# Selective-scan groups of a hybrid decoder block: VectorE order, y_diag order, and the engine of the rstd diagonals

## Chip, core and metric

One core of a Trainium2 chip runs the whole block: TensorE (PE), VectorE (DVE), ScalarE (ACT) and GpSimd (POOL) each work through a queue of their own in order, SyncE (SP) issues most transfers. The metric is the device time of one execution in microseconds (us), the median of three runs. All arithmetic is float32; the large products are made from splits, so that a float32 operand is a rounded high part plus a low part, and one product is three matmuls.

## What is computed

One decoder layer on 512 tokens of width 1024: dilated attention and a Mamba-2 mixer fed by one input projection, merged by gates, then a squared-ReLU MLP. The change is in the mixer. Its eight groups have four heads of 64 channels and a state of 128; the scan is made in four chunks of 128 tokens:

```python
def ssd_chunked(x, dt, a, bmat, cmat):
    ...
    a_cs = jnp.cumsum(la, axis=-1)
    decay = jnp.exp(jnp.where(tril, a_cs[..., :, None] - a_cs[..., None, :], -jnp.inf))
    cb = jnp.einsum('bclgn,bcsgn->bcgls', cc, bc)
    y_diag = jnp.einsum('bcghls,bcsghp->bclghp', cb[:, :, :, None] * decay, xd)
    decay_states = jnp.exp(a_cs[..., -1:] - a_cs)
    states = jnp.einsum('bclgn,bcghl,bclghp->bcghpn', bc, decay_states, xd)
    def step(hstate, inp):
        st, dec = inp
        return hstate * dec[..., None, None] + st, hstate
    _, prev = lax.scan(step, init, (states, chunk_decay))
    y_off = jnp.einsum('bclgn,bcghpn,bcghl->bclghp', cc, prev, jnp.exp(a_cs))
    return y_diag + y_off

def mamba2_mixer(...):
    ...
    y = y + d_skip * xh
    y = y * jax.nn.silu(z)
    y = y * lax.rsqrt(jnp.mean(y * y, axis=-1, keepdims=True) + RMS_EPS)   # over the 256 channels of a group
    y = y * norm_w
```

## The kernel before

The program runs through the attention, then the eight mixer groups (about 244 to 700 us), then the output projection and the MLP. In the mixer stage PE has two kinds of work. The large projections come in units of 256 columns: `x` and `bc` (inputs of the convolution of group g), `z` (its gate), `sp` (the output projection of group g-1, added into eight tiles `acc`), and at the end `gs`. A unit's weights are loaded by SP into `ws`, rounded by ACT into `wh` (L90) and the rest `wl` is taken by DVE (L93), for these units in two halves of four k-steps each; `ws`, `wh` and `wl` have two buffers each, so that a unit's split waits for the end of the last unit but one. PE results go to three banks (`psg`) for the units and five (`psa`) for the scan.

The scan of a group is `ssm_group` (L699), a generator of seven steps. `Filler.run(us)` puts matmuls of the units into PE's queue between two steps, `SSM_FILL = (2, 7, 4, 3, 9, 5, 6)` us of them for each group but the last, which has `SSM_LAST`. The steps: (1) decays `w` and `e`, loaded by a POOL transfer that repeats the cumulated decays on all partitions, then 4 exponentials for `e`, 16 Relus and one large exponential for `w` on ACT (L711 to L715); `xd` and `xs` from transposes; (2) `pb`, `pcb`, the masked `cbm` and four DVE multiplications into `w` (L746); (3) `pst`, the chunk states, and `prev`, the carried states: an ACT copy, and for two further chunks one multiplication and one addition on DVE (L758, L759); (4) for each half j `pyd` (y_diag, 16 rows in a trace), `y` (L771), `pyo` (products with the states, L773), `t1`, sum, gate (L777 to L779), square on ACT (L781), and at the end the sum of the two squares (L784); (5) `pn`, the mean of squares by matmuls, its power by POOL in `rt` (L194, L197), and diagonal matrices `dg` (L793); (6) `rg`, which spreads rstd over the partitions; (7) `yt`, the normalised result, split (L801 to L803).

PE's matmuls stand in the order in which they are written (`mm` pins them). On the other engines a scheduling layer orders the instructions by priority: the place in the code, moved ahead where `high_priority(offset)` is around it; pinned instructions keep their order among themselves. `prep` (L101) issues the next unit's load with offset 300 and splits `x`, `bc`, `z` and `sp` units with offset 0. Evacuations of projections have offset 400.

Of the kernel before, what the change touches and what calls it, by code (L numbers as in the profile page):

```python
# [77 lines left out]
def hybrid_block(ctx: ExitStack, tc: tile.TileContext, a: dict):  # L78
# [22 lines left out]
    def prep(i, offset=300, eng=None):  # L101
        if i >= len(units):
            return
        key, loads, free = units[i]
        with tc.high_priority(offset=offset):
            stage = wpool.tile([P, UF], F32, name=f"ws_{key}", tag="ws", bufs=2)
            for dst, src in loads:
                sp.dma_start(dst(stage), src)
        with tc.high_priority(offset=0 if key.rstrip("0123456789") in ("x", "bc", "z", "sp") or key == "o1" else offset):
            hi = wpool.tile([P, UF], F32R, name=f"wh_{key}", tag="wh", bufs=2)  # L110
            lo = wpool.tile([P, UF], F32R, name=f"wl_{key}", tag="wl", bufs=2)
            if key[:2] in ("up", "dn"):
                split(stage[:, :free], hi[:, :free], lo[:, :free], eng)
            else:
                for f in (slice(0, free // 2), slice(free // 2, free)):
                    split(stage[:, f], hi[:, f], lo[:, f], eng, pinned=key == "o1")
        ready[key] = (hi, lo)

    state = {"next": 0}
# [85 lines left out]
    def pin(ins):  # L205
        return tc.keep_in_program_order(ins)
# [447 lines left out]
    def h64(ap_):  # L654
        return ap_.rearrange("p (q e) -> p q e", e=64)
# [40 lines left out]

    TC = T - P

    def ssm_group(g, sz):  # L699

        xs2 = [convs.pop((g, c)) for c in range(2)]
# [6 lines left out]
        for half in range(2):  # L708
            rs_ = slice(64 * half, 64 * half + 64)
            for j in range(2):  # L710
                act.activation(e[rs_, j, :].rearrange("p (c l) -> p c l", c=3), w5[rs_, half, j, 1:, :], AF.Exp)  # L711

        for r in range(16):
            act.activation(w[:, r, :], w[:, r, :], AF.Relu, scale=-1.0, bias=acs[:, g * 16 + r : g * 16 + r + 1])
        act.activation(w, w, AF.Exp, scale=-1.0)  # L715

        xd = sg.tile([P, NT * UC], F32, name=f"xd{g}", tag="xd")
        for b in range(2):
# [32 lines left out]
        for c in range(3):  # L751
            pv = pst[c // 2][:, (c % 2) * UC : (c % 2 + 1) * UC]
            bs, us = slice(c * P, (c + 1) * P), slice(c * UC, (c + 1) * UC)
            three(pv, bk[0][:, bs], bk[1][:, bs], xsp[0][:, us], xsp[1][:, us], True, True)
        act.activation(prev[:, 0, :], pst[0][:, 0:UC], AF.Copy)
        for c in (1, 2):
            pv = pst[c // 2][:, (c % 2) * UC : (c % 2 + 1) * UC]
            dve.tensor_tensor(h64(prev[:, c, :]), h64(prev[:, c - 1, :]), bc64(cd, g, c, c + 1), op=ALU.mult)  # L758
            dve.tensor_tensor(prev[:, c, :], prev[:, c, :], pv, op=ALU.add)  # L759
        yield  # L760

        ys, sq = [], []
        for j in range(2):
            pyd = abank(f"pyd{g}_{j}")
            for c in range(NT):
                for half in range(2):
                    h = 2 * j + half
                    mm(pyd[64 * half : 64 * half + 64, c * P : (c + 1) * P],
                       xd[:, c * UC + h * 64 : c * UC + (h + 1) * 64], w[:, c * HG + h, :], start=True, stop=True)
            y = sg.tile([P, T], F32, name=f"y{g}_{j}", tag="y", bufs=2)  # L770
            dve.scalar_tensor_tensor(y, xs2[j], dskip[:, 2 * g + j : 2 * g + j + 1], pyd, op0=ALU.mult, op1=ALU.add)  # L771
            pyo = abank(f"pyo{g}_{j}")
            for c in range(1, NT):  # L773
                mm(pyo[:, (c - 1) * P : c * P], prev[:, c - 1, j * P : (j + 1) * P], ct[:, c * P : (c + 1) * P],
                   start=True, stop=True)
# [12 lines left out]
        for c in range(NT):
# [298 lines left out]
```

## Time and profile before

| | |
|---|---|
| Median of 3 runs | 1122.25 us (1120.26 to 1123.79) |
| The profiled execution | 1122.04 us, its span 1120.3 us |
| PE matmuls busy | 1094.8 us, 98% of the span |
| DVE busy | 670.7 us, 60% |
| ACT busy | 482.2 us, 43% |
| Granted TensorE clock, mean | 0.997 |

The span is what the profile shows of the execution; 1.7 us lie around it. Busy shares are over the whole span. In the mixer stage a group takes 54.6 us from one `pn` to the next. A row of the timeline gives start, duration, engine, line, operation and, in brackets, the idle time just before and what ended it.

### The profile page before, as it was taken

Reading aid. Unit: us, or ns where it says so; the run is one execution under the profiler, and the core shown is the slowest. Engines: PE = TensorE matmul, PEld = TensorE weight load, DVE = VectorE, ACT = ScalarE, POOL = GpSimd, SP = SyncE. Lnnn points to the kernel's source line nnn. Section 1 sums busy time; section 2 is a strip of 40 time slices with the busy share of each in tenths; the row PEclk is TensorE's granted clock in tenths of the full one; section 3 lists DMA queues with packets and bytes.
Section 4 is the critical chain, followed back from the end, with each engine's and each line's share of the span. In section 5 each row is a group of like instructions: output and inputs, shape, how many; then the busy total and the mean of one; then the engine's idle time right before and its main releaser. Section 6 shows DMA issues by size and latency. Waiting matters only on the chain.

```text
span 1120.3 us, 13600 instructions
## 1 busy us (share of the span) xinstructions
PE 1094.8 (98%) x5501; PEld 909.5 (81%) x5501; DVE 670.7 (60%) x986; ACT 482.2 (43%) x803; POOL 63.4 (6%) x71
## 2 busy tenths in 40 slices
PE   6999999999999999999999999999999999999997
PEld 6988877778888787878787878889888888888886
DVE  5657665347786869696969685855433234333324
ACT  6256665463556363637272623443322233232321
POOL 2203222000000000000000000000000000000000
PEclk9999999999999999999999999999999999999999
DMA  8232212332333232332323222450332324223212
GB/s 274 77 114 77 69 45 66 104 94 77 112 97 129 76 113 80 108 100 89 113 75 113 76 76 77 187 188 1 113 113 75 113 86 159 102 86 114 75 38 75
DMA packets 86463, 110.86 MB, mean 99 GB/s; under 512 B 4080, under 2 KB 74224, under 8 KB 85376
## 3 DMA queue, kind: packets, MB, share of 16 engines
q1 hardware_dynamic: 85072, 101.01, 28.2%
q0 software_dynamic: 1328, 8.98, 2.1%
q8 instruction: 43, 0.70, 0.3%
q14 instruction: 20, 0.16, 0.0%
HBM read 107.81 MB, written 2.16 MB: 98 GB/s over the span
## 4 chain that ended last, share of the span: by engine, by line
PE 89%; DVE 7%; DMA 2%; issue 1%; ACT 1%; SPq 0%; POOL 0%; POOLq 0%; DVEq 0%; ACTq 0%
PE psu L209 16%; PE psd L209 15%; PE psx L209 8%; PE psbc L209 8%; PE psz L209 8%; PE pssp L209 5%; PE psga L209 4%; PE psgs L209 4%; PE psq L209 3%; PE psk L209 3%; PE psap L209 3%; PE psv L209 3%; PE pq L209 1%; PE po L209 1%; PE pt L212 1%; DVE acc L679 1%
## 5 line engine op out<-in xcount | busy, mean ns | idle before, releaser
L209 PE MATMUL psu<-fh,wh_up 128*128 128x512 f32 (+1 forms) x288 | 105.4, 366 | 0.0
L209 PE MATMUL psu<-fl,wh_up 128*128 128x512 f32 (+1 forms) x288 | 105.2, 365 | 0.0
L209 PE MATMUL psu<-fh,wl_up 128*128 128x512 f32 (+1 forms) x288 | 105.2, 365 | 0.0
L209 PE MATMUL psd<-wl_dn,hh 128*128 128x512 f32 x240 | 93.4, 389 | 0.0
L209 PE MATMUL psd<-wh_dn,hl 128*128 128x512 f32 x240 | 93.4, 389 | 0.0
L209 PE MATMUL psd<-wh_dn,hh 128*128 128x512 f32 x240 | 93.4, 389 | 0.0
L93 DVE TENSOR_TENSOR wl_up<-ws_up,wh_up 128x2048 fp32r<-128x2048 f32 x16 | 36.7, 2292 | 77.6 <-ACT wh_up L90 77.5
L93 DVE TENSOR_TENSOR hl<-hidden,hh 128x512 fp32r<-128x512 f32 x32 | 21.9, 693 | 77.3 <-ACT hh L90 77.2
L90 ACT ACTIVATE hh<-hidden 128x512 fp32r<-128x512 f32 x32 | 20.2, 632 | 103.1 <-PE psd L209 97.6
L209 PEld LDWEIGHTS psu<-fh,wh_up 128*128 128x128 f32 x288 | 54.3, 189 | 8.8
L209 PEld LDWEIGHTS psu<-fh,wl_up 128*128 128x128 f32 x288 | 54.3, 189 | 8.7
L209 PEld LDWEIGHTS psu<-fl,wh_up 128*128 128x128 f32 x288 | 54.3, 189 | 8.7
L90 ACT ACTIVATE wh_up<-ws_up 128x2048 fp32r<-128x2048 f32 x16 | 30.7, 1916 | 61.4 <-PE psu L209 56.1
L209 PEld LDWEIGHTS psd<-wh_dn,hh 128*128 128x128 f32 x240 | 45.0, 188 | 9.5
L209 PEld LDWEIGHTS psd<-wh_dn,hl 128*128 128x128 f32 x240 | 45.0, 188 | 9.4
L209 PEld LDWEIGHTS psd<-wl_dn,hh 128*128 128x128 f32 x240 | 45.0, 188 | 9.3
L209 PE MATMUL psx<-uh,wh_x 128*128 128x512 f32 x128 | 52.4, 410 | 0.0
L209 PE MATMUL psz<-uh,wh_z 128*128 128x512 f32 x128 | 51.1, 399 | 0.0
L209 PE MATMUL pssp<-yth,wh_sp 128*128 128x512 f32 x128 | 51.0, 399 | 0.0
L209 PE MATMUL psbc<-uh,wh_bc 128*128 128x512 f32 x128 | 50.8, 397 | 0.0
L209 PE MATMUL psz<-uh,wl_z 128*128 128x512 f32 x128 | 50.1, 392 | 0.0
L209 PE MATMUL pssp<-yth,wl_sp 128*128 128x512 f32 x128 | 50.1, 392 | 0.0
(271 smaller groups left out, 2792.4 us busy)
## 6 DMA issues: line engine op xcount, KB each, us to landing
ws_up<-in_w_up_dram SPq DMA_DIRECT2D x16, 1024.0 KB, 5.4
ws_dn<-in_w_down_dram SPq DMA_DIRECT2D x15, 1024.0 KB, 5.0
ws_z<-in_w_in_dram SPq DMA_DIRECT2D x8, 1024.0 KB, 5.2
ws_x<-in_w_in_dram SPq DMA_DIRECT2D x8, 1024.0 KB, 5.2
w<-acs_d POOLq DMA_DIRECT2D x8, 1024.0 KB, 5.0
ws_bc<-in_w_in_dram SPq DMA_DIRECT2D x16, 512.0 KB, 4.7
ws_sp<-in_w_ssm_proj_dram SPq DMA_DIRECT2D x8, 1024.0 KB, 4.8
ws_ga<-in_w_in_dram SPq DMA_DIRECT2D x4, 1024.0 KB, 5.3
```

What stands on the lines that cost most here:

```text
L90: ins = act.activation(hi, src, AF.Copy)
L93: (eng or dve).tensor_tensor(lo, src, hi.bitcast(F32), op=ALU.subtract)
L209: tc.keep_in_program_order(pe.matmul(*args, **kw))
L212: tc.keep_in_program_order(pe.transpose(dst, src, ident))
L679: dve.tensor_tensor(acc[o], acc[o], ps, op=ALU.add)
```

## The change

Five edits, all for the mixer stage. The carried states `prev` are put 200 places ahead on ACT and DVE, and their four DVE instructions pinned. The split of the `x` unit (all but the first) is held back (`held`) until the states are written, and its low halves are pinned, so that they stand behind the states in DVE's queue. Both `pyd` halves are issued ahead of the two `pyo`. The decays of group g+1 (`decays`) are written at the end of step 4 of group g, pinned on ACT; the squares are pinned too. The diagonals `dg` are made by four ACT copies with a scale in place of one DVE multiplication.

```diff
+        if key[0] == "x" and key != "x0":
+            held.append(lambda: split_unit(key, stage, free, eng, 0, True))
+        else:
+            split_unit(key, stage, free, eng,
+                       0 if key.rstrip("0123456789") in ("x", "bc", "z", "sp") or key == "o1" else offset)
...
-        (eng or dve).tensor_tensor(lo, src, hi.bitcast(F32), op=ALU.subtract)
+        ins = (eng or dve).tensor_tensor(lo, src, hi.bitcast(F32), op=ALU.subtract)
+        if lo_pinned:
+            tc.keep_in_program_order(ins)
...
+    def decays(g):
...
-                act.activation(e[rs_, j, :].rearrange("p (c l) -> p c l", c=3), w5[rs_, half, j, 1:, :], AF.Exp)
+                pin(act.activation(e[rs_, j, :].rearrange("p (c l) -> p c l", c=3), w5[rs_, half, j, 1:, :], AF.Exp))
...
-        act.activation(w, w, AF.Exp, scale=-1.0)
+        pin(act.activation(w, w, AF.Exp, scale=-1.0))
+        ws_e[g] = w, e
+
+    def ssm_group(g, sz):
+
+        xs2 = [convs.pop((g, c)) for c in range(2)]
+        w, e = ws_e.pop(g)
...
-        act.activation(prev[:, 0, :], pst[0][:, 0:UC], AF.Copy)
-        for c in (1, 2):
-            pv = pst[c // 2][:, (c % 2) * UC : (c % 2 + 1) * UC]
-            dve.tensor_tensor(h64(prev[:, c, :]), h64(prev[:, c - 1, :]), bc64(cd, g, c, c + 1), op=ALU.mult)
-            dve.tensor_tensor(prev[:, c, :], prev[:, c, :], pv, op=ALU.add)
+        with tc.high_priority(offset=200):
+            act.activation(prev[:, 0, :], pst[0][:, 0:UC], AF.Copy)
+            for c in (1, 2):
+                pv = pst[c // 2][:, (c % 2) * UC : (c % 2 + 1) * UC]
+                pin(dve.tensor_tensor(h64(prev[:, c, :]), h64(prev[:, c - 1, :]), bc64(cd, g, c, c + 1), op=ALU.mult))
+                pin(dve.tensor_tensor(prev[:, c, :], prev[:, c, :], pv, op=ALU.add))
+        while held:
+            held.pop()()
         yield
...
+        pyds = [abank(f"pyd{g}_{j}") for j in range(2)]
         for j in range(2):
-            pyd = abank(f"pyd{g}_{j}")
             for c in range(NT):
                 for half in range(2):
                     h = 2 * j + half
-                    mm(pyd[64 * half : 64 * half + 64, c * P : (c + 1) * P],
+                    mm(pyds[j][64 * half : 64 * half + 64, c * P : (c + 1) * P],
                        xd[:, c * UC + h * 64 : c * UC + (h + 1) * 64], w[:, c * HG + h, :], start=True, stop=True)
+        for j in range(2):
             y = sg.tile([P, T], F32, name=f"y{g}_{j}", tag="y", bufs=2)
...
-            act.activation(q, y, AF.Square, scale=1.0 / math.sqrt(UC))
+            pin(act.activation(q, y, AF.Square, scale=1.0 / math.sqrt(UC)))
...
+        if g + 1 < GROUPS:
+            decays(g + 1)
         yield
...
-        dve.tensor_tensor(dg, ident.unsqueeze(1).broadcast_to([P, NT, P]), rt.unsqueeze(2).broadcast_to([P, NT, P]),
-                          op=ALU.mult)
+        for c in range(NT):
+            with tc.high_priority(offset=100):
+                act.activation(dg[:, c, :], ident, AF.Copy, scale=rt[:, c : c + 1])
```

What that makes of the queues is shown for group 2 (names carry the group: `w2`, `prev2`; `wl_x3` and `wl_bc3` are weight splits of group 3; line numbers are those of the kernel the rows are of). Groups 3 to 6 read alike. First DVE where the carried states are made, before:

```order
L746 TENSOR_TENSOR w2_3170<-w2_3170,cbm2_3263 128x512 x2
L93 TENSOR_TENSOR wl_x3_3278<-ws_x3_3275,wh_x3_3277 128x1024
L679 TENSOR_TENSOR acc2_2890<-acc2_2890,pssp1_2_3299 128x512
L679 TENSOR_TENSOR acc3_2899<-acc3_2899,pssp1_3_3324 128x512
L93 TENSOR_TENSOR wl_x3_3278<-ws_x3_3275,wh_x3_3277 128x1024
L758 TENSOR_TENSOR prev2_3303<-prev2_3303,cd_92 128x256
L771 SCALAR_TENSOR_TENSOR y2_0_3345<-ct4_3019,dskip_171,pyd2_0_3336 128x512
L759 TENSOR_TENSOR prev2_3303<-prev2_3303,pst2_0_3304 128x256
L758 TENSOR_TENSOR prev2_3303<-prev2_3303,cd_92 128x256
L759 TENSOR_TENSOR prev2_3303<-prev2_3303,pst2_1_3305 128x256
L777 TENSOR_TENSOR t12_0_3351<-pyo2_0_3347,e2_3172 128x384
```

DVE at the same place in the changed kernel:

```order
L764 TENSOR_TENSOR w2_2954<-w2_2954,cbm2_3269 128x512
L777 TENSOR_TENSOR prev2_3303<-prev2_3303,cd_92 128x256
L764 TENSOR_TENSOR w2_2954<-w2_2954,cbm2_3269 128x512
L691 TENSOR_TENSOR acc2_2893<-acc2_2893,pssp1_2_3299 128x512
L778 TENSOR_TENSOR prev2_3303<-prev2_3303,pst2_0_3304 128x256
L691 TENSOR_TENSOR acc3_2902<-acc3_2902,pssp1_3_3330 128x512
L777 TENSOR_TENSOR prev2_3303<-prev2_3303,cd_92 128x256
L778 TENSOR_TENSOR prev2_3303<-prev2_3303,pst2_1_3305 128x256
L93 TENSOR_TENSOR wl_x3_3321<-ws_x3_3281,wh_x3_3320 128x1024 x2
L793 SCALAR_TENSOR_TENSOR y2_0_3360<-ct4_3046,dskip_171,pyd2_0_3342 128x512
L799 TENSOR_TENSOR t12_0_3366<-pyo2_0_3362,e2_2956 128x384
```

The states have moved ahead of the fourth `w`, of two `acc` and of both halves of the `x` split. Then DVE at the end of step 4, up to the sum of squares that `pn` reads, before:

```order
L777 TENSOR_TENSOR t12_1_3372<-pyo2_1_3368,e2_3172 128x384
L679 TENSOR_TENSOR acc5_2960<-acc5_2960,pssp1_5_3383 128x512
L778 TENSOR_TENSOR y2_1_3366<-y2_1_3366,t12_1_3372 128x384
L779 SCALAR_TENSOR_TENSOR y2_1_3366<-y2_1_3366,sz2_1_3272 128x512
L679 TENSOR_TENSOR acc6_2969<-acc6_2969,pssp1_6_3391 128x512
L784 TENSOR_TENSOR sq2_0_3355<-sq2_0_3355,sq2_1_3376 128x512
```

And in the changed kernel:

```order
L691 TENSOR_TENSOR acc7_3005<-acc7_3005,pssp1_7_3429 128x512
L799 TENSOR_TENSOR t12_1_3378<-pyo2_1_3374,e2_2956 128x384
L93 TENSOR_TENSOR wl_bc3_3441<-ws_bc3_3437,wh_bc3_3440 128x1024
L800 TENSOR_TENSOR y2_1_3372<-y2_1_3372,t12_1_3378 128x384
L93 TENSOR_TENSOR wl_bc3_3441<-ws_bc3_3437,wh_bc3_3440 128x1024
L801 SCALAR_TENSOR_TENSOR y2_1_3372<-y2_1_3372,sz2_1_3278 128x512
L806 TENSOR_TENSOR sq2_0_3370<-sq2_0_3370,sq2_1_3382 128x512
L206 TENSOR_SCALAR rt2_3476<-pn2_3471 128x4
```

Both halves of the `bc` split and the last `acc` now stand ahead of the sum of squares. Third, ACT from the squares of group 2 on (`e3`, `w3` decays of group 3; `ch`, `ct` convolution; `dg2` the diagonals), before:

```order
L781 ACTIVATE sq2_1_3376<-y2_1_3366 128x512
L711 ACTIVATE e3_3599<-w3_3597 64x384
L90 ACTIVATE wh_bc3_3410<-ws_bc3_3407 128x1024 x2
L711 ACTIVATE e3_3599<-w3_3597 64x384 x3
L714 ACTIVATE w3_3597<-w3_3597,acs_93 128x128 x8
L641 ACTIVATE ch6_3451<-psx3_0_3416,cb_167,cw_165 128x512
L714 ACTIVATE w3_3597<-w3_3597,acs_93 128x128 x8
L715 ACTIVATE w3_3597<-w3_3597 128x2048
L646 ACTIVATE ct6_3456<-ch6_3451 128x512
L90 ACTIVATE wh_z3_3496<-ws_z3_3494 128x1024
L641 ACTIVATE ch7_3486<-psx3_1_3459,cb_167,cw_165 128x512
L90 ACTIVATE wh_z3_3496<-ws_z3_3494 128x1024
```

ACT in the changed kernel, from the first conv of group 3 on (`wh_bc3` and `sq2_1` stand ahead of it):

```order
L653 ACTIVATE ch6_3484<-psx3_0_3446,cb_167,cw_165 128x512
L723 ACTIVATE e3_3387<-w3_3385 64x384
L819 ACTIVATE dg2_3479<-ident_63,rt2_3476 128x128 x4
L723 ACTIVATE e3_3387<-w3_3385 64x384 x2
L726 ACTIVATE w3_3385<-w3_3385,acs_93 128x128
L658 ACTIVATE ct6_3489<-ch6_3484 128x512
L726 ACTIVATE w3_3385<-w3_3385,acs_93 128x128 x10
L653 ACTIVATE ch7_3519<-psx3_1_3492,cb_167,cw_165 128x512
L726 ACTIVATE w3_3385<-w3_3385,acs_93 128x128 x5
L90 ACTIVATE wh_z3_3529<-ws_z3_3527 128x1024
L727 ACTIVATE w3_3385<-w3_3385 128x2048
L658 ACTIVATE ct7_3524<-ch7_3519 128x512
```

The diagonals have come into the queue ahead of nearly all decays of the next group, and the `z` split behind the second convolution has moved behind them. POOL's and SP's queues read alike in both kernels; PE's differs by the swapped `pyd` and `pyo` alone.

## Rows read from the trace of the kernel before

**Rows 1.** Page, part 1: busy time, share, instructions

```profile
PE 1094.8 (98%) x5501; PEld 909.5 (81%) x5501; DVE 670.7 (60%) x986; ACT 482.2 (43%) x803; POOL 63.4 (6%) x71
```

**Rows 2.** PE's waits: for whom, total us, times, longest

```profile
PE pyo L209 <- DVE prev L759: 9.6, 11, 1.4
```

**Rows 3.** Timeline of PE, group 1: the projections' matmuls around step 4

```profile
333.80 0.39 PE L209 MATMUL pssp<-yth,wl_sp 128*128 128x512 f32 x1
...
337.73 0.48 PE L209 MATMUL pssp<-yth,wh_sp 128*128 128x512 f32 x1
```

**Rows 4.** Timeline of PE, group 2: step 4

```profile
385.57 0.39 PE L209 MATMUL pssp<-yth,wl_sp 128*128 128x512 f32 x1
...
388.61 0.49 PE L209 MATMUL pyo<-ct,prev 128*128 128x128 f32 x2 [1.21 <-DVE prev L759]
...
389.53 0.49 PE L209 MATMUL pyo<-ct,prev 128*128 128x128 f32 x2 [0.43 <-DVE prev L759]
...
391.66 0.48 PE L209 MATMUL pssp<-yth,wh_sp 128*128 128x512 f32 x1
```

**Rows 5.** Timeline of DVE, group 2: third `w` to the sum of squares

```profile
382.48 1.29 DVE L746 TENSOR_TENSOR w<-w,cbm 128x512 f32<-128x512 f32 x2
...
383.68 1.22 DVE L93 TENSOR_TENSOR wl_x<-ws_x,wh_x 128x1024 fp32r<-128x1024 f32 x1
...
389.05 0.42 DVE L759 TENSOR_TENSOR prev<-prev,pst 128x256 f32<-128x256 f32 x1
...
396.61 0.69 DVE L784 TENSOR_TENSOR sq<-sq,sq 128x512 f32<-128x512 f32 x1
```

**Rows 6.** Timeline of PE: `pn` of groups 2 and 3

```profile
402.00 0.95 PE L209 MATMUL pn<-ones,sq 128*128 128x1 f32 x8
...
456.64 0.95 PE L209 MATMUL pn<-ones,sq 128*128 128x1 f32 x8
```

**Rows 7.** DVE by line and shape: busy us, mean ns, idle before

```profile
L679 DVE TENSOR_TENSOR acc<-acc,pssp 128x512 f32<-128x512 f32 x48 | 32.4, 683 | 3.9 <-PE pssp L209 3.7
L93 DVE TENSOR_TENSOR wl_bc<-ws_bc,wh_bc 128x1024 fp32r<-128x1024 f32 x16 | 19.0, 1222 | 3.0 <-ACT wh_bc L90 2.9
```

**Rows 8.** Timeline of ACT and DVE, group 2: after `pn`

```profile
400.27 2.45 ACT L714 ACTIVATE w<-w,acs 128x128 f32<-128x128 f32 x8
...
404.37 0.69 DVE L793 TENSOR_TENSOR dg<-ident,rt 128x512 f32<-128x512 f32 x1 [1.22 <-POOL rt L197]
...
414.88 0.78 ACT L641 ACTIVATE ch<-psbc,cb,cw 128x512 f32<-128x512 f32 x1 [3.03 <-PE psbc L209]
```

**Rows 9.** Timeline of DVE, group 3: `cbm`

```profile
433.06 0.68 DVE L742 TENSOR_TENSOR cbm<-pcb,tri 128x512 f32<-128x512 f32 x1
```

**Rows 10.** ACT by line and shape: busy us, mean ns, idle before

```profile
L90 ACT ACTIVATE wh_bc<-ws_bc 128x1024 fp32r<-128x1024 f32 x16 | 16.1, 1047 | 2.2 <-PE psap L209 1.8 <-PE pssp L209 0.4
L715 ACT ACTIVATE w<-w 128x2048 f32<-128x2048 f32 x8 | 15.3, 1916 | 0.2
```

**Rows 11.** Timeline of PE, group 1: `pn`; chain that ended last, `bc` unit of group 2

```profile
348.02 0.95 PE L209 MATMUL pn<-ones,sq 128*128 128x1 f32 x8
...
354.70 10.92 PE psbc L209 x48
```

**Rows 12.** Timeline of DVE and PE, group 0: last state, first `wl_x` matmul

```profile
285.36 0.42 DVE L759 TENSOR_TENSOR prev<-prev,pst 128x256 f32<-128x256 f32 x1
...
286.12 0.39 PE L209 MATMUL psx<-uh,wl_x 128*128 128x512 f32 x1
```

**Rows 13.** Timeline of PE, group 7; granted clock of a stretch (column PEclk)

```profile
661.51 0.39 PE L209 MATMUL pssp<-yth,wl_sp 128*128 128x512 f32 x1
...
665.19 0.49 PE L209 MATMUL pyo<-ct,prev 128*128 128x128 f32 x2 [1.44 <-DVE prev L759]
...
668.75 0.66 PE L209 MATMUL pssp<-yth,wh_sp 128*128 128x512 f32 x1
...
665.60:668.70 3.10, 3.10 (x23) 2.76 (x23) 2.49 (x5) 0.00 (x0) 0.00 (x0) 0.52 0.00 0
```

More of the change, by code (lines that the diff above doesn't have):

```diff
@@ L86, in hybrid_block, with split @@
     dram = ctx.enter_context(tc.tile_pool(name="dram", bufs=1, space=DRAM))
-    def split(src, hi, lo, eng=None, pinned=False):
+    def split(src, hi, lo, eng=None, pinned=False, lo_pinned=False):
         ins = act.activation(hi, src, AF.Copy)
@@ L108, in prep, with split_unit @@
                 sp.dma_start(dst(stage), src)
-        with tc.high_priority(offset=0 if key.rstrip("0123456789") in ("x", "bc", "z", "sp") or key == "o1" else offset):
+        if key[0] == "x" and key != "x0":
[3 more added lines that the diff above has]
+                       0 if key.rstrip("0123456789") in ("x", "bc", "z", "sp") or key == "o1" else offset)
+    held = []
+    def split_unit(key, stage, free, eng, offset, lo_pinned=False):
+        with tc.high_priority(offset=offset):
             hi = wpool.tile([P, UF], F32R, name=f"wh_{key}", tag="wh", bufs=2)
@@ L115, in prep @@
                 for f in (slice(0, free // 2), slice(free // 2, free)):
-                    split(stage[:, f], hi[:, f], lo[:, f], eng, pinned=key == "o1")
+                    split(stage[:, f], hi[:, f], lo[:, f], eng, pinned=key == "o1", lo_pinned=lo_pinned)
         ready[key] = (hi, lo)
@@ L697, in hybrid_block @@
     TC = T - P
-    def ssm_group(g, sz):
-        xs2 = [convs.pop((g, c)) for c in range(2)]
+    ws_e = {}
+    def decays(g):
         w = sg.tile([P, 16, P], F32, name=f"w{g}", tag="w")
@@ L710, in ssm_group @@
             for j in range(2):
-                act.activation(e[rs_, j, :].rearrange("p (c l) -> p c l", c=3), w5[rs_, half, j, 1:, :], AF.Exp)
+                pin(act.activation(e[rs_, j, :].rearrange("p (c l) -> p c l", c=3), w5[rs_, half, j, 1:, :], AF.Exp))
         for r in range(16):
-            act.activation(w[:, r, :], w[:, r, :], AF.Relu, scale=-1.0, bias=acs[:, g * 16 + r : g * 16 + r + 1])
-        act.activation(w, w, AF.Exp, scale=-1.0)
+            pin(act.activation(w[:, r, :], w[:, r, :], AF.Relu, scale=-1.0, bias=acs[:, g * 16 + r : g * 16 + r + 1]))
+        pin(act.activation(w, w, AF.Exp, scale=-1.0))
[3 more added lines that the diff above has]
+        w, e = ws_e.pop(g)
         xd = sg.tile([P, NT * UC], F32, name=f"xd{g}", tag="xd")
@@ L767, in ssm_group @@
                     h = 2 * j + half
-                    mm(pyd[64 * half : 64 * half + 64, c * P : (c + 1) * P],
+                    mm(pyds[j][64 * half : 64 * half + 64, c * P : (c + 1) * P],
                        xd[:, c * UC + h * 64 : c * UC + (h + 1) * 64], w[:, c * HG + h, :], start=True, stop=True)
+        for j in range(2):
             y = sg.tile([P, T], F32, name=f"y{g}_{j}", tag="y", bufs=2)
-            dve.scalar_tensor_tensor(y, xs2[j], dskip[:, 2 * g + j : 2 * g + j + 1], pyd, op0=ALU.mult, op1=ALU.add)
+            dve.scalar_tensor_tensor(y, xs2[j], dskip[:, 2 * g + j : 2 * g + j + 1], pyds[j], op0=ALU.mult, op1=ALU.add)
             pyo = abank(f"pyo{g}_{j}")
@@ L827, in hybrid_block @@
         fill.add(f"gs{j}", gate_unit("gs", j))
+    decays(0)
     for g in range(GROUPS):
```

## Prediction

> **What bounds the kernel now.** I read the page first, then PE's waits, then the timeline of one mixer group. On the page the reader should see that PE is busy for 98% of the span [rows 1], so only PE's idle time, or work that it needn't do, can be won. The list of its waits names the place: 9.6 us in 11 waits, nearly all in `pyo`, for the carried states `prev` of DVE [rows 2]. The two of each of the groups 2 to 6 are in the timeline: the second chunk of `pyo` waits 1.21 us, the third 0.43 us [rows 4]. The true cost is larger than these idle times, since the pipeline drains beside them: from the last `pssp` ahead of step 4 to the first behind it 6.09 us pass in group 2 (385.57 to 391.66 [rows 4]) and 3.93 us in group 1 (333.80 to 337.73 [rows 3]), with the same matmuls and no wait. So 2.16 us a group hang on the states.
>
> DVE's queue says why: behind the third and fourth `w` (382.48) stand a half of the `x` split (383.68, 1.22 us), two `acc`, the other half, and only then the states, of which the last starts at 389.05 [rows 5]. DVE was not short of time in the whole, it did other things first.
>
> **The change, part by part.** The sum is made against the profiled execution's own 1122.04 us (span 1120.3); the median, 1122.25, is 0.2 us above it.
>
> *States ahead, `x` split behind, both `pyd` first.* I walk DVE's queue of group 2 in its new order. Two instructions that don't need each other follow at 0.60 us for 512 columns (two `w` take 1.29 [rows 5], and `acc` has a mean of 0.68 [rows 7]); a split half counts 1.14 (1.22 less the same overlap [rows 7]); a state 0.45 (0.42 and a short wait [rows 5]); a 384-wide one 0.5, an estimate in proportion. The third `w` ends at 383.1. Then four states, one `w` and two `acc`, 3.6 us, and 0.2 for ACT's copy of the first state: 386.9. PE, with both `pyd` first, wants the last state at about 388, so the wait there is gone with 1 us to spare.
>
> *What is late next.* The `x` split now stands between the states and step 4's sums, and the `bc` split, 2.3 us, has come ahead of the sum of squares. From 386.9: the `x` split 2.3, eight 512-wide (two `y`, four `acc`, two gates) 4.8, four 384-wide 2.0, the `bc` split 2.3: 398.3; 0.3 for two `acc` that wait for their matmuls, 0.75 for ACT's last square, 0.69 for the sum [rows 5]: 400.1. Before, that sum ended at 397.3 [rows 5] and `pn` stood at 402.00 [rows 6], with 4.7 us of cover. Now PE comes to `pn` 2.16 us earlier, at 399.84, and waits 0.3. Group 2 wins 1.85 of the 2.16 us.
>
> *The loop behind `pn`.* From now on PE and DVE are tied: `pn` waits for the sum, and through `rt`, `dg` and ACT's queue the sum of the next group waits for `pn`. `dg` could start 2.37 us behind `pn` (402.00 [rows 6], 404.37 [rows 8]), at 402.5. Then ACT has, in one stretch: 4 `dg` and 16 Relus of 0.29 (eight in 2.45 us [rows 8]), two `e` of 0.5, the large exponential 1.85 (1.92 less overlap [rows 10]), one split half 1.0 [rows 10], and four of the convolution at 0.65 (0.78 less overlap [rows 8], the tanh a little less): 5.8 + 1.0 + 1.85 + 1.0 + 2.6 = 12.25, to 414.75. In the kernel before, that last one ended at 415.66, having waited 3.03 us for PE [rows 8]; so ACT's slack there is used up, and the DVE work behind it comes 0.9 us earlier, where PE is 1.85 us earlier. `cbm` of the next group falls at 432.15 in place of 433.06 [rows 9]. From `cbm` to the end of its sum: `cbm`, three `w`, a gate, two `acc`, 4.2, and the 16.6 us just walked without the wait for the copy and half the others: 452.9. Period 452.9 - 400.1 = 52.8 us, against 54.64 before (402.00 to 456.64 [rows 6]) and 52.5 that PE alone needs (54.64 - 2.16). Groups 3 to 6 win 1.85 us each, 7.4.
>
> *`dg` on ACT.* DVE loses one instruction of 0.69 [rows 8], ACT gains four, 1.2 us. `rg` stands 5 us of other matmuls behind `pn` in PE's queue (the sixth number of `SSM_FILL`), and `dg` is there 3.6 us behind it: covered by 1.4 us. Queued behind the waiting `dg` on ACT are the decays, the next convolution and the `z` split; that is the stretch above. If the cover were gone, PE would pay at `rg`, 1 us for 1 us. The Trainium skill (ScalarE: Activation LUTs, Rules for kernel authors) says to use VectorE, not ScalarE, for a multiplication; by it `dg` would stay on DVE, ACT's stretch would be 1.2 us shorter, DVE's 0.6 longer, and the period would be PE's 52.5, 0.3 us a group better than mine.
>
> *Decays earlier on ACT.* 21 activations a group as before, the POOL transfer too, and POOL's and SP's queues read alike. In one place they stand in the way: behind group 1, `wh_bc2` has its first half behind `dg1` and its second behind the large exponential and a convolution. `pn` there is at 348.02 [rows 11]; `dg` at 350.4 plus 1.2, two Relus 0.6, half a split 1.0, tanh 0.6, exponential 1.85, convolution 0.7, half a split 1.0 [rows 8, 10]: 357.35. DVE then, two convolutions first, 1.3, overlapping, and 1.2 for `wl_bc2`: about 358.9 to 359.3. PE starts that unit at 354.70 [rows 11] and wants the low second half 14 matmuls of 0.227 later, 357.9. It waits 1.0 to 1.4 us, once: I take 1.2, ends 0 and 2.
>
> *Group 0.* Here PE has three matmuls of `psx` ahead of `pyd`, the third reading `wl_x1` at 286.12 [rows 12]. The half it reads now comes behind the last state, 285.78 [rows 12], and 1.22 us later it is 287.0: PE waits 0.85 us. Group 0 and 1 had no wait to lose.
>
> *Group 7.* Its stretch took 7.24 us (661.51 to 668.75 [rows 13]), 3.31 above group 1's. Part is a wait of 1.4 us, part a lower clock: after it PE was granted 0.52 of full speed for 3.1 us [rows 13], near the lower of its two levels. In the new order two `w` stand behind the states. By the durations above the fourth `w` would end some 0.8 us after `pyd` wants it, and DVE comes another 0.9 us late against PE, as in the loop: a new wait of 1.7 us, an estimate. It wins 1.6, ends 0 and 3.3.
>
> *Sum.* -0.85 (group 0), 1.85 - 1.2 (group 2), 7.4 (3 to 6), 1.6 (7): 8.8 us. 1122.04 - 8.8 = 1113.2 us. The attention and the MLP read the same in both kernels' queues.
>
> **The rivals.**
> *PE alone sets the pace.* My periods are sums of some sixty durations; if ACT's and DVE's stretch is 0.3 us shorter, `pn` doesn't wait. Then 5 x 2.16 and 3.31, less the waits of groups 0 and 2 that my walk may have too long: 14.1, that is 1107.9 us. Back-to-back `pyd` of one shape could make it a little better. For it: DVE is idle 40% [rows 1]. Against: no idle DVE time lies between `w` and the sum.
>
> *The wait moves to `pn` nearly whole.* If each of the 22 instructions between states and sum costs 0.07 us more, the period is 54.3: groups 3 to 6 win 0.35 each, group 2 the same less 1.2, group 0 loses 0.85, group 7 wins 1.6. In all 0.9 to 1.5, 1120.8 us. It would also be the outcome if the states came 1 us later than walked, so that `pyo` went on waiting.
>
> *ACT's queue becomes the bound, and the kernel slower.* `dg` waits at the head of ACT's queue for POOL's power, with the decays pinned behind it and the second half of the `z` split behind the exponential and two convolutions. In my walk that stretch is full. From 1.85 us more in it (a `dg` of 0.75 us each would do) the period passes 54.64; at 2.5 us more it is 55.3, five groups lose 0.65 each, groups 0 and 2 lose 2.05, group 7 wins 1.6: 1122.04 + 3.7 = 1125.7 us. For it: the 3.03 us that ACT idled there are gone [rows 8]. Against: the 128-wide Relus, the same shape, cost 0.29.
>
> **How the numbers follow.** Chances: forecast 0.60, PE alone 0.20, wait moved to `pn` 0.14, ACT the bound 0.06. The measurement can tell about 0.3%, 3.4 us, from no change, so faster means below 1118.9. Forecast and PE alone lie there, and a quarter of the third case, which spreads from 1117 to 1122: faster 0.84, same 0.10, slower 0.06. The forecast's own ends are 1109 (group 7 at 3.3, no wait in groups 0 and 2) and 1117 (loop 0.8 us longer). The range of 8 in 10 takes in most of PE alone and the lower part of the third case: 1106.0 to 1118.5.
>
> **What the profile after would show.** No wait of `pyo` for `prev`, or tenths; in its place a wait of `pn` for the sum (`sq`), 0 to 0.6 us in groups 2 to 6; 52.5 to 53 us from `pn` to `pn`; one wait in `psbc` of group 2 and one in `psx` of group 0, about 1 us each; `rg` without a wait; in group 7 a wait of `pyd` for `w`, and no stretch at half clock. I am wrong if `pn` waits over 1.5 us in each group, if `psz` waits for `wl_z`, or if `pyo` still waits for the states.

## The result, and the profile after

The changed kernel takes 1113.87 us in the median of 6 runs (1113.51 to 1114.33), the kernel before, beside it on the same chip, 1121.15 us: a ratio of 0.9929, with a 95% interval of 0.9918 to 0.9941. That is 7.3 us, 0.7%, faster; the forecast was 1113.2 us. The profiled execution took 1114.33 us, its span is 1112.6 us, against 1120.3 us before; the mean granted clock is 0.998. PE is still busy for 98% of a shorter span (page, part 1, to be read against [rows 1]):

```profile
PE 1090.3 (98%) x5501; PEld 905.4 (81%) x5501; DVE 663.0 (60%) x978; ACT 488.8 (44%) x835; POOL 63.3 (6%) x71
```

PE's waits after (for whom, total us, times, longest). The eleven of [rows 2] are gone, and smaller ones have come elsewhere:

```profile
PE ut L224 <- DVE un L321: 9.7, 3, 7.4
PE pn L221 <- DVE sq L806: 2.7, 5, 0.5
PE psbc L221 <- DVE wl_bc L93: 1.5, 2, 1.0
PE psx L221 <- DVE wl_x L93: 0.7, 1, 0.7
PE pyd L221 <- DVE w L764: 0.6, 2, 0.4
PE psbc L221 <- ACT wh_bc L90: 0.4, 1, 0.4
```

The first, in `ut`, belongs to the start of the program and is outside the change. The others are all new: five of `pn` for the sum of squares, three of `psbc` in one place, one of `psx`, two of `pyd`.

Step 4 of group 2 after, the stretch of [rows 4]. It runs from 389.43 to 393.00, 3.57 us in place of 6.09, and no state is waited for. It is also shorter than the 3.93 us of [rows 3], where nothing waited either:

```profile
389.43 0.39 PE L221 MATMUL pssp<-yth,wl_sp 128*128 128x512 f32 x1
389.75 1.97 PE L221 MATMUL pyd<-w,xd 128*64 128x128 f32 x32
391.64 1.60 PE L221 MATMUL pyo<-ct,prev 128*128 128x128 f32 x12
393.00 0.48 PE L221 MATMUL pssp<-yth,wh_sp 128*128 128x512 f32 x1
```

The `pn` of groups 0, 1, 2, 6 and 7 after (timeline of PE). They cut the mixer into pieces that can be set against before, where they stood at 300.34, 348.02 [rows 11], 402.00 [rows 6], 620.56 and 679.24. Each `pn` has eight matmuls; a smaller count is the part that fell into the stretch asked for:

```profile
301.21 0.95 PE L221 MATMUL pn<-ones,sq 128*128 128x1 f32 x8
...
348.59 0.61 PE L221 MATMUL pn<-ones,sq 128*128 128x1 f32 x5
...
404.04 0.61 PE L221 MATMUL pn<-ones,sq 128*128 128x1 f32 x4 [0.54 <-DVE sq L806]
...
615.91 0.83 PE L221 MATMUL pn<-ones,sq 128*128 128x1 f32 x6 [0.54 <-DVE sq L806]
...
671.90 0.83 PE L221 MATMUL pn<-ones,sq 128*128 128x1 f32 x7
```

| Piece | Forecast, us won | Measured, us won | From |
|---|---|---|---|
| up to `pn` of group 0 | -0.85 | -0.87 | 300.34, 301.21 |
| group 0 to 1 | 0 | 0.30 | 47.68, 47.38 |
| group 1 to 2 | 1.85 - 1.2 = 0.65 | -1.47 | 53.98, 55.45 |
| group 2 to 6 | 7.4 | 6.69 | 218.56, 211.87 |
| group 6 to 7 | 1.6 | 2.69 | 58.68, 55.99 |
| behind | 0 | 0.36 | rest of the spans |
| sum | 8.8 | 7.7 | 1120.3, 1112.6 |

Two pieces need an explanation, group 1 to 2 and the 6.69. In the second, the period is 211.87 / 4 = 52.97 us. What ties it is in the chain that ended last (start, us, engine, tile), from the `pssp` behind step 4 of group 3 to the `pn` of that group:

```profile
446.21 4.83 PE pssp L221 x21
...
451.07 0.07 DVE acc L691
...
451.67 0.55 DVE t L799
452.22 1.13 DVE wl_bc L93
...
453.82 1.14 DVE wl_bc L93
454.96 0.61 DVE y L801
...
456.26 0.70 DVE sq L806
...
457.01 1.05 PE pn L221 x8
```

The last `acc` on DVE waits for PE's last `pssp`; behind it stand `t`, the two halves of the `bc` split (2.27 us), the gate and the sum. PE has only matmuls of `psx` to do meanwhile and is idle for 0.54 us in front of `pn`. In the first piece, group 1 to 2, ACT's queue is the place to look (timeline of ACT):

```profile
345.76 0.53 ACT L723 ACTIVATE e<-w 64x384 f32<-64x384 f32 x1 [3.33 <-DMA w<-acs_d]
...
352.93 1.27 ACT L819 ACTIVATE dg<-ident,rt 128x128 f32<-128x128 f32 x4
...
358.62 1.05 ACT L90 ACTIVATE wh_bc<-ws_bc 128x1024 fp32r<-128x1024 f32 x1
```

The first `e` of group 2, pinned ahead, waits 3.33 us for the load of `w2`; all decays and `dg1` come behind it, and `wh_bc2` behind them. In the groups behind it no `e` waits for its load, and there the issue times differ: POOL issues `w` ahead of SP's load `ws_z`, also 1 MB (392.25 and 392.99 in group 2), where in group 1 it comes behind it (337.50 and 336.68) and `e` starts 8.3 us later. PE then stops three times in the `bc` unit, for 0.40, 0.53 and 1.02 us (timeline of PE):

```profile
355.78 0.50 PE L221 MATMUL psbc<-uh,wh_bc 128*128 128x512 f32 x1 [0.40 <-ACT wh_bc L90]
...
357.04 0.50 PE L221 MATMUL psbc<-uh,wl_bc 128*128 128x512 f32 x1 [0.53 <-DVE wl_bc L93]
...
361.47 0.50 PE L221 MATMUL psbc<-uh,wl_bc 128*128 128x512 f32 x1 [1.02 <-DVE wl_bc L93]
```

### The profile page after: what moved, and what is told of

Its sections match the earlier page's. It is cut to its first block, busy times and chain, and to the rows that moved or that the text cites. A ratio compares the mean times of both kernels' runs of the same rounds, so it can differ in the third digit from the quotient of the medians.

```text
span 1112.6 us, 13596 instructions
## 1 busy us (share of the span) xinstructions
PE 1090.3 (98%) x5501; PEld 905.4 (81%) x5501; DVE 663.0 (60%) x978; ACT 488.8 (44%) x835; POOL 63.3 (6%) x71
## 3 DMA queue, kind: packets, MB, share of 16 engines
HBM read 107.81 MB, written 2.16 MB: 99 GB/s over the span
## 4 chain that ended last, share of the span: by engine, by line
PE 92%; DVE 3%; ACT 2%; DMA 1%; issue 1%; SPq 0%; POOL 0%; POOLq 0%; DVEq 0%; ACTq 0%
PE psu L221 16%; PE psd L221 15%; PE psz L221 8%; PE psbc L221 8%; PE pssp L221 7%; PE psx L221 4%; PE psga L221 4%; PE psgs L221 4%; PE psq L221 3%; PE psk L221 3%; PE psv L221 3%; PE psap L221 3%; PE psp L221 2%; PE pso L221 2%; PE pq L221 1%; PE pyd L221 1%
## 5 line engine op out<-in xcount | busy, mean ns | idle before, releaser
L221 PE MATMUL psbc<-uh,wl_bc 128*128 128x512 f32 x128 | 50.1, 391 | 1.5 <-DVE wl_bc L93 1.5
L221 PE MATMUL psx<-uh,wl_x 128*128 128x512 f32 x128 | 50.0, 391 | 0.7 <-DVE wl_x L93 0.7
```

Source lines behind the costliest of these rows:

```text
L221: tc.keep_in_program_order(pe.matmul(*args, **kw))
```

## The experiments

The theory after this reading: (1) the states' place ahead of the `x` split is the win, and the grouped `pyd` saves only changes of shape; (2) the `bc` split ahead of the sum sets the period; (3) the load in front of the pinned decays makes the stall of group 2; (4) `dg` on ACT is not needed for any of it. The rivals: the order of the halves is the win; `dg` or ACT's queue sets the period. As a measure free of the program's start, the table at the end of this section has the time from `pn` of group 1 to `pn` of group 7, taken from PE's timeline of each run.

### The old order of the halves, the rest as changed

```diff
-        pyds = [abank(f"pyd{g}_{j}") for j in range(2)]
+        pyds = [None, None]
         for j in range(2):
+            pyds[j] = abank(f"pyd{g}_{j}")
             ...
-        for j in range(2):
             y = sg.tile([P, T], F32, name=f"y{g}_{j}", tag="y", bufs=2)
```

> The changed kernel with one part undone: the products with the states again follow each y_diag half (pyd0, pyo0, pyd1, pyo1). Theory (the states' place in VectorE's queue made the win, the order of the halves only saves shape changes): prev is ready when pyo0 starts, step 4 of group 2 takes 3.9 us in place of 3.57, and in groups 2 to 6 most of that hides in the wait of pn for the sum of squares (0.54 us each), so 0.4 to 2 us slower than the changed kernel: 1114.3 to 1115.9 us. Rival (the order of the halves made the win, since it gives the states 1 us more of cover): the waits of pyo for prev come back, 1.2 to 1.6 us in each of six groups, 1121 to 1124 us.

Measured: 1113.71 us, ratio to before 0.9934 (0.9918 to 0.9951), so no difference from the changed kernel that can be told. No `pyo` waits for a state, so the rival falls: the states' place removes those waits without the grouped halves. But the quiet total hides two effects. Step 4 takes 3.92 us (386.41 to 390.33 in PE's timeline of group 2), 0.35 more, and all of it shows in the period, 53.3 us; the wait of `pn` did not absorb it, as I had expected, since the `acc` in front of the sum moves with PE:

```profile
401.33 1.05 PE L221 MATMUL pn<-ones,sq 128*128 128x1 f32 x8 [0.54 <-DVE sq L806]
...
454.60 1.05 PE L221 MATMUL pn<-ones,sq 128*128 128x1 f32 x8 [0.54 <-DVE sq L806]
```

Against that, the stall of group 2 is gone: in this order of ACT's queue the first half of `wh_bc2` happens to stand ahead of `e2`, and none of `psbc`'s three waits appears. 0.35 us a group lost and 2.98 us won once (`pn` of group 1 to 2 in 52.47 us, 55.45 in the changed kernel) nearly cancel.

### The decays behind the `bc` split

```diff
-        if g + 1 < GROUPS:
-            decays(g + 1)
         yield
+        if g + 1 < GROUPS:
+            with tc.issue_after(bc_act[-1].ins), tc.issue_after(sq_act[-1].ins):
+                decays(g + 1)
```

`bc_act` holds ACT's second half of the last `bc` split, `sq_act` the last square; the decays of group 0 stay pinned, the others are held by these two alone.

> The changed kernel with the decays of group g+1 queued on ScalarE behind the second half of the bc weight split and behind the squares of group g; in the queues this moves only wh_bc2 ahead of e2 and what follows from it. Theory (psbc of group 2 starved because e2 at the head of ScalarE's queue waited 3.33 us for the load of w2, with wh_bc2 behind it): the three waits of psbc2 (0.40, 0.53, 1.02 us) go, and 2.5 to 3.3 us are won against the changed kernel: 1110.6 to 1111.4 us. Rival (wh_bc2 was late because dg and the decays fill ScalarE): under 0.7 us won, 1113.2 to 1114.5 us.

Measured: 1110.81 us, 0.9909 (0.9894 to 0.9924), 3.1 us less than the changed kernel. Both halves of `wh_bc2` now run while the load is under way, `e2` waits 0.62 us for it instead of 3.33 (timeline of ACT), and no `psbc` waits:

```profile
341.94 1.06 ACT L92 ACTIVATE wh_bc<-ws_bc 128x1024 fp32r<-128x1024 f32 x1
...
345.05 1.89 ACT L730 ACTIVATE e<-w 64x384 f32<-64x384 f32 x4 [0.62 <-DMA w<-acs_d]
```

This shows that the stall is `wh_bc2`'s place in ACT's queue. It can't tell the load from `dg1` and the decays, as its two expectations were meant to, since the split now stands ahead of all of them.

### The `bc` split behind the sum of squares

```diff
+        elif key[:2] == "bc" and sums:
+            with tc.issue_after(sums[-1].ins):
+                split_unit(key, stage, free, eng, 0)
...
-        dve.tensor_tensor(sq[0], sq[0], sq[1], op=ALU.add)
+        sums.append(dve.tensor_tensor(sq[0], sq[0], sq[1], op=ALU.add))
```

> The changed kernel with the low halves of the bc weight split of groups 3 to 7 queued on VectorE behind the sum of squares of the group before. Theory (the period of groups 2 to 6 is 52.97 and not that of TensorE alone because two splits of 1.2 us stand ahead of the sum): the sum comes about 2.4 us earlier, the five waits of pn (2.7 us in all) go, the period falls to 52.1 to 52.5, and 2.5 to 4.3 us are won against the changed kernel: 1109.6 to 1111.4 us. Rival (ScalarE's queue, with dg on it, sets the period): pn or the rstd product waits as before, period 52.9 to 53.0, 1113.2 to 1114.5 us.

Measured: 1110.0 us, 0.9902 (0.9887 to 0.9917), 3.9 us less than the changed kernel. In group 2 the sum starts at 401.10, 2 us before PE comes to `pn`, and the split follows (timeline of DVE):

```profile
401.10 0.69 DVE L809 TENSOR_TENSOR sq<-sq,sq 128x512 f32<-128x512 f32 x1 [0.70 <-ACT sq L806]
401.71 2.35 DVE L93 TENSOR_TENSOR wl_bc<-ws_bc,wh_bc 128x1024 fp32r<-128x1024 f32 x2
```

`pn` comes at 403.17 without a wait, and in the chain that ended last one `pn` follows the other by 52.11 us:

```profile
403.33 0.79 PE pn L224 x8
...
455.44 0.79 PE pn L224 x8
```

Reading (2) holds: 0.86 us a group (52.97 - 52.11) were the `bc` split's, though `pn` showed only 0.54 us of idle time for it. `dg` was on ACT throughout.

### `dg` on DVE again

```diff
-        for c in range(NT):
-            with tc.high_priority(offset=100):
-                act.activation(dg[:, c, :], ident, AF.Copy, scale=rt[:, c : c + 1])
+        dve.tensor_tensor(dg, ident.unsqueeze(1).broadcast_to([P, NT, P]), rt.unsqueeze(2).broadcast_to([P, NT, P]),
+                          op=ALU.mult)
```

> The changed kernel with one part undone: the diagonals dg again as one product on VectorE. Theory (dg has time on either engine, and the ends are set by the sum of squares): the period of groups 2 to 6 stays within 0.15 us of 52.97, and the time within 1 us of the changed kernel, 1112.9 to 1114.9 us, if anything less, since ScalarE has 1.2 us less ahead of wh_bc2 in group 1. Rival (dg on ScalarE carried part of the win, because on VectorE it holds the convolutions while it waits for GpSimd): the period rises by 0.5 us or more, 1116 to 1121 us.

Measured: 1111.74 us, 0.992 (0.9903 to 0.9936), 2.1 us less than the changed kernel, below what I expected. The period is 52.94 us, so the engine of `dg` has nothing to do with it; but the stall of group 2 is gone here too. `e2` waits for the load as before (3.31 us), yet without `dg1` the second half of `wh_bc2` starts 2.5 us earlier, at 356.11 in place of 358.62 (timeline of ACT), and that is early enough for every `psbc`:

```profile
356.11 1.05 ACT L90 ACTIVATE wh_bc<-ws_bc 128x1024 fp32r<-128x1024 f32 x1
```

`dg1` is 1.27 us of these 2.5; the rest is a tanh and a convolution that stood ahead of the split and now stand behind it (357.06 and 357.58). So the load's wait by itself doesn't stall PE, and reading (3) was only half of it: the wait and `dg` with what stands around it are too long only together. No run takes the load's wait alone away; its share is argued.

### The grouped `pyd` alone, on the kernel before

```diff
+        pyds = [abank(f"pyd{g}_{j}") for j in range(2)]
         for j in range(2):
-            pyd = abank(f"pyd{g}_{j}")
             ...
+        for j in range(2):
             y = sg.tile([P, T], F32, name=f"y{g}_{j}", tag="y", bufs=2)
```

> The kernel before with one part of the change alone: both y_diag halves ahead of the products with the states; the states stay behind the x split on VectorE, dg stays there, the decays are not pinned. Theory: 1 us more cover for the states takes most of the waits of pyo (1.64 us a group) away, but in the queue of ScalarE three of the e of the next group now stand ahead of the first square, and they wait for the load of w, which can't be issued before the second y_diag half is done and takes 8 us; so the squares and the sum come later and pn waits instead: 1119 to 1125 us. Rival (the order alone is the win, nothing new waits): 6 x 1.4 us and 0.4 us of shape changes in eight groups won, 1110 to 1113.5 us.

Measured: 1117.95 us, 0.9974 (0.9964 to 0.9984): faster, by less than half of the change, and between my two expectations. PE's waits (total us, times, longest):

```profile
PE pyo L209 <- DVE prev L759: 7.3, 11, 1.0
PE pn L209 <- DVE sq L785: 1.7, 2, 1.0
```

The waits of `pyo` fall only from 9.6 to 7.3 us, since DVE also takes the second `y` in between, now that its `pyd` is ready. The other half of the theory is there but mostly covered: ACT stands for 12.88 us before an `e` that the load of `w3` ends, the squares come behind it, and DVE is idle for 3.92 us in front of the sum. Before, `pn` had 4.7 us of cover [rows 5, 6], and it is used up in two groups only, for 1.04 us in group 5 and 0.70 in group 6. From `pn` to `pn` it is 54.05 us in groups 2 to 4, then 55.24 and 56.53. ACT in group 2:

```profile
395.24 1.47 ACT L711 ACTIVATE e<-w 64x384 f32<-64x384 f32 x3 [12.88 <-DMA w<-acs_d]
```

### The states ahead alone, on the kernel before

The edits to `prep`, `split_unit` and `prev` are kept as in the change; the halves, `dg`, the decays and the squares are as before.

```diff
+        with tc.high_priority(offset=200):
+            act.activation(prev[:, 0, :], pst[0][:, 0:UC], AF.Copy)
...
+        while held:
+            held.pop()()
```

> The kernel before with one part of the change alone: the carried states ahead of the x split on VectorE; old order of the halves, dg on VectorE, decays and squares not pinned. Theory (a load at the head of ScalarE's queue is as bad as a split at the head of VectorE's): the waits of pyo for prev go, but in ScalarE's queue the e of the next group and some of its Relu now stand ahead of the second square, and they wait for the load of w, which is issued when the second y_diag half is done and takes about 8 us: the second square ends about 403 us in group 2, pn waits 2.5 to 4 us a group, period 55 to 57 us, 1121 to 1130 us. Rival (the pinning of decays and squares is only a precaution; the states' place is the whole win): no wait at pn over 0.6 us, period 53.0 to 53.5 us, 1111 to 1114.5 us.

Measured: 1147.84 us, 1.0246 (1.023 to 1.0261): slower by 2.5%, the direction expected and far more of it. No `pyo` waits. The chain that ended last shows what does (group 2, start and us): the load of `w3` first, then everything that ACT has queued between it and the second square.

```profile
391.46 8.32 DMA w<-acs_d
...
400.16 1.99 ACT wh_bc L90 x2
...
403.95 1.28 ACT w L726 x4
405.22 0.53 ACT sq L804
...
405.78 0.70 DVE sq L807
```

`pn` waits 4.53 us, and then PE runs at the lower of its two clock levels: 0.50 is granted from 406.5 to 412.0, where it was 1.00 ahead of the wait (timeline row of PE; then two windows, column PEclk after the busy times):

```profile
406.52 1.87 PE L221 MATMUL pn<-ones,sq 128*128 128x1 f32 x8 [4.53 <-DVE sq L807]
```

```profile
406.50:409.50 3.00, 2.98 (x11) 2.79 (x12) 0.82 (x2) 3.00 (x11) 0.75 (x1) 0.50 0.60 244
409.50:412.00 2.50, 2.50 (x7) 1.92 (x7) 2.10 (x3) 2.05 (x3) 0.28 (x1) 0.50 0.01 3
```

Behind these windows it is 0.50 from 412 to 413 and 0.94 from 413 to 415, so that half the clock lasts some 1.2 us longer. The period is 60.0 us (406.52 to 466.49), 6.7 more than with the same order of the halves and everything pinned (53.3, with `dg` on ACT). 4.0 us are more wait; the rest, 2.7 us, is put down to the clock, the part that I had left out. By an estimate, some 6.7 us at half the clock are worth 3.3 us, so the two do not add up exactly.

### Nothing pinned, the rest as changed

```diff
-                pin(act.activation(e[rs_, j, :].rearrange("p (c l) -> p c l", c=3), w5[rs_, half, j, 1:, :], AF.Exp))
+                act.activation(e[rs_, j, :].rearrange("p (c l) -> p c l", c=3), w5[rs_, half, j, 1:, :], AF.Exp)
...
-            pin(act.activation(q, y, AF.Square, scale=1.0 / math.sqrt(UC)))
+            act.activation(q, y, AF.Square, scale=1.0 / math.sqrt(UC))
...
-        if g + 1 < GROUPS:
-            decays(g + 1)
```

The decays are called at the start of `ssm_group` again.

> The changed kernel with one part undone: decays and squares not pinned, the decays written at the start of their group as before; the states ahead, the grouped halves and dg on ScalarE stay. Theory (the pinning is what makes the states' new place pay): as in the run of the states alone, two Relu of the next group, both bc splits, the four e and five more Relu stand ahead of the second square on ScalarE, and the first of them waits for the load of w; pn waits 4 to 6 us a group, period 58 to 60 us, 1135 to 1148 us. Rival (the run of the states alone was slow for its old order of the halves or its dg): waits of pn under 1 us, 1110 to 1116 us.

Measured: 1122.74 us (1118.41 to 1129.02 in 10 runs), 1.001 (0.9991 to 1.0029): the whole gain is gone, though neither expectation holds in size. The second square stands behind nearly the same queue as in the run of the states alone. But the load of `w3` is issued at 388.93 instead of 391.46, and in group 2 its wait on ACT is 0.29 us instead of 4.02; in group 5 it is 1.92 (timeline of POOL, then of ACT):

```profile
388.93 0.59 POOL L716 DMA_DIRECT2D w<-acs_d  x1 [38.23 <-PE pyo L221]
```

```profile
394.30 0.70 ACT L726 ACTIVATE w<-w,acs 128x128 f32<-128x128 f32 x2 [0.29 <-DMA w<-acs_d]
...
559.03 0.70 ACT L726 ACTIVATE w<-w,acs 128x128 f32<-128x128 f32 x2 [1.92 <-DMA w<-acs_d]
```

The earlier issue is the smaller part: counted from `pn` of group 1 (348.21 here, 350.07 there) it is 0.7 us. The load is also faster, 5.4 us in place of 8.3, and so are the medians of all eight (page, part 6, the states alone and then this run; KB each, us to landing):

```profile
w<-acs_d POOLq DMA_DIRECT2D x8, 1024.0 KB, 8.2
```

```profile
w<-acs_d POOLq DMA_DIRECT2D x8, 1024.0 KB, 5.3
```

Here `w` is issued 0.74 us ahead of `ws_z` (389.67), there 0.29 us behind it (391.17), and the median of `ws_z` is 7.3 us here and 6.7 there. That this order makes the difference is likely, but not shown: the two runs differ in the engine of `dg` too, and no run swaps the two loads alone.

`pn` waits 1.05 to 3.01 us, 8.3 us in five groups, and behind three of these waits the granted clock falls to about half (0.50 from 511 to 513, for one). So the pinning, which reads like a precaution, and the earlier place of the decays, undone with it here, are needed for the gain as much as the states' new place. The grouped halves seem to matter here for a reason that I had not seen: with them the load of `w` goes ahead of `ws_z`.

### Three edits together, and the same with `dg` on DVE

The decays behind the `bc` split, the `bc` split behind the sum (both as above), and for the stall of group 0:

```diff
-        if key[0] == "x" and key != "x0":
+        if key[0] == "x" and key not in ("x0", "x1"):
```

> The changed kernel with three edits together: the decays behind the bc split on ScalarE, the low halves of the bc split behind the sum of squares on VectorE, and the x split of group 1 not held (the place where psx waits 0.69 us for it). Theory (three waits, each with its own cause): what each gives adds up, 3.1 us and 3.9 us as measured by themselves and 0.5 to 0.7 us for the third: 1105.8 to 1107.2 us, period 52.1 us, and no wait of psx, psbc or pn left between group 0 and group 6. Rival (they share slack, and with two gone the third's gain is hidden or something new waits, as ScalarE's dg behind four of the Relu): 1108 to 1110 us.

Measured: 1105.64 us, 0.9863 (0.9848 to 0.9878). This beats both kernels: 15.6 us under the kernel before beside it. What is left of PE's waits besides the start is `pyd` in group 7, 0.6 us. In the chain that ended last, one group is matmuls and nothing else from `pn` to `pn`:

```profile
399.29 0.79 PE pn L229 x8
...
445.95 5.44 PE psx L229 x24
451.39 0.67 PE pn L229 x7
```

The period is 52.1 us (399.12 to 451.23). From `pn` of group 1 to that of group 7 the three edits give 7.6 us, where the two alone gave 3.3 and 4.1: they add up. The time is 0.2 us under the range that I expected, within the scatter of the runs.

> The kernel of the three edits together with dg as one product on VectorE again. Theory (with the bc split out of the way, nothing waits for dg, and its engine does not matter): period 52.1 us, 1105.2 to 1106.1 us, the same as the three edits with dg on ScalarE. Rival (dg on VectorE waits 1.2 us for GpSimd in front of the convolutions, and psbc or the rstd product starts to wait; or, the other way, ScalarE's 1.27 us still cost something): over 0.8 us apart.

Measured: 1105.74 us, 0.9859 (0.9844 to 0.9874), the same. Moving `dg` to ACT gives nothing, once nothing else leans on ACT's queue, and it cost about 2 us in the changed kernel.

| Kernel | Median us | `pn` of group 1 to group 7, us | Period, us |
|---|---|---|---|
| before | 1121.15 | 331.22 | 54.64 |
| changed | 1113.87 | 323.31 | 52.97 |
| old order of the halves | 1113.71 | 322.04 | 53.3 |
| decays behind the `bc` split | 1110.81 | 320.00 | 52.97 |
| `bc` split behind the sum | 1110.0 | 319.23 | 52.11 |
| `dg` on DVE | 1111.74 | 320.42 | 52.94 |
| grouped `pyd` alone | 1117.95 | 329.25 | 54.05 to 56.5 |
| states ahead alone | 1147.84 | 355.15 | 60.0 |
| nothing pinned | 1122.74 | 330.75 | 53.5 to 57.0 |
| three edits | 1105.64 | 315.72 | 52.1 |
| three edits, `dg` on DVE | 1105.74 | 315.71 | 52.1 |

## Why the prediction was right, point by point

*What bounds the kernel.* Right. PE set the pace, the states' place in DVE's queue was the wait, and the runs confirm it from both sides: with the states ahead no `pyo` waits in either order of the halves, with the order alone three quarters of the wait stay. One reading was off: beside those 9.6 us PE's waits before have 9.2 us of `ut` (three, the longest 7.8), so "nearly all" holds of the mixer and not of the program.

*The win of step 4.* Under-sized: 2.16 us forecast, 2.52 measured (6.09 to 3.57). The forecast took group 1 as the floor; equal shapes side by side save another 0.35 us, which the run with the old order gives back exactly. It also explains the 0.30 us of group 0 to 1, forecast at 0. The Trainium skill (TensorEngine Tiling (Array Packing), Key Properties) says that a change of the tiling mode drains the engine. The trace agrees: `pyd` works with 128*64 tiles and `pyo` with 128*128, and two changes fewer make 3.57 us of 3.92; the drain itself no row shows.

*What is late next.* The kind was right, the `bc` split ahead of the sum makes `pn` wait, and the run with the split moved shows it. The size was 0.3 us and is 0.86.

*The loop behind `pn`.* The number came out, 52.8 forecast and 52.97 measured, but by luck and not by the step that was to give it: PE alone needs 52.1 and not 52.5, and the wait costs 0.86 and not 0.3. I tied the groups through `rt`, `dg` and ACT's stretch; with `dg` off ACT the period is the same, 52.94, and the chain shows the tie in another place, PE's last `pssp`, the `acc` that waits for it on DVE, and the `bc` split behind that. The walk was right about which instructions stand in front of the sum and wrong about where their start hangs.

*`dg` on ACT.* "Covered" was right for `rg`, which never waits. The step gave the four copies no price beyond `rg`; that they stand in front of `wh_bc2` is counted only in the next one. The Trainium skill (ScalarE: Activation LUTs, Rules for kernel authors) says to use VectorE, not ScalarE, for a multiplication. The run with `dg` on VectorE agrees, 2.1 us faster, but not in the way that I had worked out: it was to bring the period to 52.5, which stayed at 52.94, and the gain was the stall of group 2.

*Decays earlier on ACT.* This is the step that failed in size: 1.2 us with ends 0 and 2, measured about 3.1 (2.52 won in step 4 less 0.86 at `pn`, and 1.47 lost in all). The mechanism, `wh_bc2` behind `dg1` and the decays, was right. Left out was the head of that queue: the first `e` needs the load of `w2`, issued at the end of step 4 and 8.3 us under way, so the whole queue came 3.3 us late at its head, and `dg1` started 4.3 us behind `pn` (348.59 to 352.93) in place of the 2.4 us of the walk. I had read the moved transfer in POOL's queue as unchanged, and did not ask who now stands waiting for it.

*Group 0.* Right in the wait: 0.85 forecast, and `psx` is 1.10 us late (287.22 less 286.12 [rows 12]), of which 0.25 us is a later start of the whole mixer, which I didn't trace. That `pn` is 0.87 us late is luck: the 0.25 us are nearly made up by 0.23 us that step 4 gives back here.

*Group 7.* Under-sized: 1.6 forecast, 2.69 measured. The stretch takes 4.62 us (656.95 to 661.57) in place of 7.24. The new wait for `w` was put at 1.7 us; it is 0.6 us of idle time, and 1.05 us by the stretch against group 2's 3.57. As there, 0.35 us more come from the shapes; the stretch at half the clock of [rows 13] is gone, as forecast (0.52 before, 1.00 after, column PEclk):

```profile
658.90:663.00 4.10, 4.03 (x38) 3.65 (x39) 3.96 (x8) 0.00 (x0) 0.00 (x0) 1.00 0.00 0
```

*The rivals.* "PE alone" did not happen in the changed kernel, but it is what the three edits reach, at 52.1 us a group and not 52.5. "ACT's queue becomes the bound" did not happen in the whole but did in one place, group 2. What no rival named is that the pinning could be needed at all: without it, and with the decays back at their old place, the change is worth nothing.

So the forecast's 8.8 us against 7.7 by the spans is made of an error of -2.1 in group 2, -0.7 in groups 3 to 6, and +1.1, +0.3 and +0.4 in group 7, group 1 and behind. That these partly cancel is luck. Left open is the 0.36 us behind group 7, which I didn't trace.

## What to carry to other kernels

When instructions are moved ahead on an in-order engine, look at the first of them and ask for the slowest thing it waits for, a load above all; its wait is handed to everything queued behind it, on this engine and then on the others, and whatever has no slack left there pays it. Look too at which of two loads is issued first. When one wait is removed, move out of the way also what now stands between the last input from PE and the result that PE wants next: weight splits, which are needed much later, belong behind it. And undo the parts of a change one at a time: here one part gave nothing and cost 2 us, another looked like a precaution and the gain needed it, and two opposite effects of the same size hid in a run that seemed to change nothing.

## What the runs showed of the hardware

The same load of `w`, 1 MB repeated over the partitions, took 8.3 us from its issue to the next activation in one run (391.46 to 399.78) and 5.4 us in another (388.93 to 394.30); in the first SP's 1 MB load `ws_z` was issued 0.29 us before it, in the second 0.74 us behind it. I had taken no number for it.

A wait of PE of 4.53 us was followed by some 6.7 us with about 0.50 of the clock granted, one of 1.44 us in the kernel before by 3.1 us with 0.52 [rows 13], while behind each of the five waits of 0.54 us of the changed kernel 1.00 was granted for 7 us. The length of the one wait does not decide it: with nothing pinned 1.00 stayed behind waits of 1.38 and 1.84 us (401.56 and 455.82), and 0.50 came behind one of 1.05 us (509.28).

Changing between the tile shapes of `pyd` and `pyo` two times more a group cost 0.35 us.
